# Moving 56 modulation tiles between the stages of a one-core diffusion/mLSTM layer

## The chip, the core and the metric

The kernel runs on one core of one Trainium2 chip. The metric is the device time of one execution in microseconds (us). A core has five engines that run their own instruction streams in order and wait for each other by semaphores: PE (matmul; its weight loads are shown apart as PEld), DVE (VectorE), ACT (ScalarE), POOL (GpSimd) and SP (SyncE, used here only to issue transfers). An instruction at the head of a stream that waits for something holds up everything behind it in that stream.

## The reference

One layer over 128 context tokens and 512 latent tokens (T = 640, width D = 1024) in fp32. Nine modulation vectors per conditioning row come from one small product; every other step uses some of them:

```python
def adaln(cvec, w, b):                       # w (D, 9*D); two rows: c_ctx and c
    m = jax.nn.silu(cvec) @ w + b
    return m.reshape(cvec.shape[0], N_MOD, D_MODEL)

def layer(x, mods, l, p, ctx):
    hh = rmsnorm(x, g[0]) * (1 + m[1]) + m[0]
    x = x + 0.5 * m[2] * swiglu(hh, ffn1_w1, ffn1_w3, ffn1_w2)     # first half-step
    hh = rmsnorm(x, g[1]) * (1 + m[4]) + m[3]
    y, ctx_out = token_mixer(hh, p, l, ctx)                        # attention || mLSTM
    x = x + m[5] * y
    hh = rmsnorm(x, g[2]) * (1 + m[7]) + m[6]
    x = x + 0.5 * m[8] * swiglu(hh, ffn2_w1, ffn2_w3, ffn2_w2)     # second half-step
```

`token_mixer` projects `hh` to everything at once, normalises and rotates the attention's queries and keys, runs differential softmax attention with 8 heads, and a chunkwise mLSTM with 4 heads in both directions (5 chunks of 128 tokens, with a matrix state C that each chunk updates); each branch is gated and both are projected out.

## The kernel before, in words

Everything is kept feature-major: x is 8 tiles of 128 features by 640 tokens, handled as two halves of 320 tokens (`hf` 0 and 1). fp32 products are made from three products of split operands: a high part (names ending in H) and the remainder (L). A weight tile arrives as `raw`, ACT copies it to the H part, and DVE subtracts to get the L part (L123 and L39 in attention and mLSTM, L283/L265 and L39 in the half-steps, whose tiles are called `wB`, `wC` and `ww`). PE cannot start on a weight tile before DVE's subtraction is done. The weights' `raw` tiles come from a ring of two buffers.

The stages, in order: a start in which m0 and m1 are made on PE; the first half-step (up-projections, then down-projections in 28 products numbered `i`; each product has places `at` = 0 and 1 between its parts); the second norm; projections of q, k, v with rotation; attention, head by head (`hd` 0 to 7), each in five score steps (`qi` 0 to 4); the mLSTM, head by head, in ten cells each (five chunks, two directions); the output projection; the second half-step. Independent projections ("fill units" of 24 matmuls each, `Fill`) are threaded between the dependent steps of attention and mLSTM to keep PE occupied.

The modulation vectors m2 to m8 aren't made on PE. They are 56 "tiles", each a 128x1024 piece of the weight that is loaded (512 KB, `raw_a` or `ada`) and multiplied with the two conditioning rows (`csil`, kept replicated on all 128 partitions, 1 MB) and summed along its rows on DVE: two instructions at L626 per tile, one for each row. `Columns.tile()` emits one tile, `Columns.place(n, csil, load)` says from where the next n tiles take their buffers. `columns.then` makes the derived scales when a vector's eight tiles are done. Where the tiles are put is what the change edits:

- in the first half-step `modulation(i, at)` puts one tile at `at` = 1 of products 2 to 17, and one more at `at` = 0 of products 4 and 12 (18 tiles). From product 20 on (the last part of the down phase, which needs no up-projection) there is one at `at` = 0 and two at `at` = 1 of each of eight products (24 tiles); there `csil`, `junk` and the loaded tiles sit in the buffers of tags B and C, those of the weight parts `wB` and `wC`
- in attention the loop over heads puts one tile behind the scores of `qi` 1 and 3 of heads 0 to 5, and one more at `qi` 2 of heads 2 and 4 (14 tiles). `csil` is loaded again there, into the buffers of two later mLSTM operands.

Four other things sit at the places that the change touches. `Stats.add` squares x (`nsq`) on ACT and sums the eight squares into `nacc` on DVE for the second norm; for the second half of the tokens its tag is `nt`, which the norm of the first half (`norm_apply`, `nt`, `hH`, `hL`) uses at that time too. `gate_products` loads and splits the weights of the mLSTM's gates (`wgH` L981, `wgL`), and `gate_rows` turns their product `ps_g` into gate rows. `Head.pack` splits a head's queries (`qpk`, L1160 on ACT, then a subtraction on DVE) and copies its keys (`kpk`, L1164); `queries` then transposes `qpk` on PE (`ps_qkT`) and makes the keys' remainder, and `keys` transposes the keys. The residual x is loaded again at product 18.

The program's text is written once in dependency order; a scheduler at build time orders each engine's instructions, with `tc.issue_after(ins)` as a lower bound on where a block may be put. DMA waits in the stream of SP count: SP issues in order, and a load whose buffer isn't free stands in front of all later loads.

## Time and profile before

| | before |
|---|---|
| time, median of 3 runs | 1912.65 us (1911.35 to 1914.5) |
| the profiled execution | 1915.8 us, of which the profile's span is 1914.0 us |
| PE busy | 1817.3 us, 95% of the span, 12,622 matmuls |
| DVE busy | 1330.7 us, 70% |
| ACT busy | 856.7 us, 45% |
| mean granted TensorE clock | 0.981 |
| moved by DMA | 304.68 MB, 159 GB/s over the span |

"Busy" is the time in which an engine had an instruction in it. A row of the timeline view has the start and duration, the engine, the line and operation, the tiles (out<-in), and in square brackets how long the engine stood idle just before and which instruction ended that wait. The windows view gives the busy time of each engine in a stretch, with the granted clock of TensorE (PEclk; 1.00 is full speed, 0.93 over 25 us means 3.5 us at half speed) and the share of time the DMA engines were busy.

### The profile page before, as it was taken

To read this page: it belongs to the slowest core of one execution; us is meant where nothing else is said; L and a number is where in the kernel's file an instruction comes from. 1 tells how busy PE (TensorE), PEld (TensorE's weight loads), DVE (VectorE), ACT (ScalarE), POOL (GpSimd) and SP (SyncE) were. 2 spreads that over 40 slices of the span, in tenths; PEclk is the share of its full clock that TensorE was granted. 3 is DMA by queue.
4 is the path that set the end of the run, shared out by engine and by line. 5 is a ranking of instruction groups with operands and counts; after the bars stand their busy time and mean duration, and the time that the engine had idled before them with its cause. 6 is when DMAs were issued, how large, how long until landed. Compare 5 with 4: busy or idle time off the path is not lost.

```text
span 1914.0 us, 30831 instructions
## 1 busy us (share of the span) xinstructions
PE 1817.3 (95%) x12622; PEld 1777.5 (93%) x12622; DVE 1330.7 (70%) x2252; ACT 856.7 (45%) x1469; POOL 50.9 (3%) x81
## 2 busy tenths in 40 slices
PE   6899999998989999999999989999999999998989
PEld 4899999997888999999999989899999999998989
DVE  7788987487777566675765545664457888886775
ACT  5644444111454454453544446555335655553332
POOL 1000001010000000000000000000000000001100
PEclk9999999998999999999999999999999999999989
DMA  8344557965414323223121353445432454557952
GB/s 321 116 144 178 181 188 265 376 208 171 153 45 159 102 72 123 76 95 104 68 103 60 107 165 92 144 162 194 176 131 79 169 182 171 179 184 266 355 209 93
DMA packets 129471, 304.68 MB, mean 159 GB/s; under 512 B 9585, under 2 KB 93041, under 8 KB 116657
## 3 DMA queue, kind: packets, MB, share of 16 engines
q1 hardware_dynamic: 115714, 241.04, 36.4%
q0 software_dynamic: 13616, 61.67, 8.7%
q8 instruction: 99, 1.62, 0.4%
q14 instruction: 42, 0.34, 0.1%
HBM read 236.10 MB, written 66.58 MB: 158 GB/s over the span
## 4 chain that ended last, share of the span: by engine, by line
PE 72%; DVE 10%; DMA 9%; issue 3%; ACT 3%; POOL 0%; SPq 0%; DVEq 0%; ACTq 0%; POOLq 0%
PE ps_f L52 29%; PE ps_p L52 21%; PE ps_t L52 11%; PE ps_o L52 2%; PE sc L52 2%; DMA g_dram<-g 2%; DMA raw<-in_w2b 2%; DMA ada<-in_w_ada_c 2%; PE ps_n L52 2%; DVE ww L39 2%; PE ps_wT L55 1%; PE ps_u L52 1%; PE ps_qkT L55 1%; DVE ada L626 1%; DVE junk L626 1%
## 5 line engine op out<-in xcount | busy, mean ns | idle before, releaser
L52 PE MATMUL ps_f<-S,ww 128*128 128x320 f32 x2052 | 333.9, 312 | 10.7 <-DVE ww L39 4.8
L52 PEld LDWEIGHTS ps_f<-S,ww 128*128 128x128 f32 x2052 | 310.9, 190 | 14.0 <-DVE ww L39 7.3
L52 PE MATMUL ps_p<-hH,wH 128*128 128x320 f32 x864 | 274.5, 318 | 3.1 <-ACT aT L1268 2.5
L52 PE MATMUL ps_p<-hL,wH 128*128 128x320 f32 x864 | 267.7, 310 | 0.0
L52 PE MATMUL ps_p<-hH,wL 128*128 128x320 f32 x864 | 267.6, 310 | 0.0
L52 PE MATMUL ps_t<-wH,hH 128*128 128x256 f32 x640 | 186.1, 291 | 0.9 <-DVE x L42 0.9
L52 PE MATMUL ps_f<-hm,wB 128*128 128x320 f32 x1128 | 182.5, 311 | 0.0
L52 PE MATMUL ps_t<-wL,hH 128*128 128x256 f32 x640 | 182.1, 285 | 0.0
L52 PE MATMUL ps_t<-wH,hL 128*128 128x256 f32 x640 | 182.0, 284 | 0.0
L39 DVE TENSOR_TENSOR ww<-raw,ww 128x2048 fp32r<-128x2048 f32 (+1 forms) x62 | 138.7, 2237 | 54.9 <-ACT ww L265 30.6
L52 PE MATMUL ps_f<-hm,ww 128*128 128x320 f32 x996 | 160.2, 313 | 12.5 <-ACT u L375 9.3
L52 PEld LDWEIGHTS ps_f<-hm,wB 128*128 128x128 f32 x1128 | 170.8, 189 | 0.0
L52 PEld LDWEIGHTS ps_p<-hH,wH 128*128 128x128 f32 x864 | 163.3, 189 | 4.3 <-ACT aT L1268 2.7
L52 PEld LDWEIGHTS ps_f<-hm,ww 128*128 128x128 f32 x996 | 151.8, 192 | 13.5 <-ACT u L375 9.9
L52 PEld LDWEIGHTS ps_p<-hL,wH 128*128 128x128 f32 x864 | 163.1, 189 | 0.5
L52 PEld LDWEIGHTS ps_p<-hH,wL 128*128 128x128 f32 x864 | 162.9, 189 | 0.0
L39 DVE TENSOR_TENSOR wL<-raw,wH 128x2048 fp32r<-128x2048 f32 x49 | 112.1, 2288 | 41.5 <-ACT wH L123 41.4
L123 ACT ACTIVATE wH<-raw 128x2048 fp32r<-128x2048 f32 x49 | 93.6, 1911 | 100.2 <-PE ps_p L52 88.7
L265 ACT ACTIVATE ww<-raw 128x2048 fp32r<-128x2048 f32 (+1 forms) x52 | 97.7, 1880 | 84.2 <-PE ps_f L52 53.7
L39 DVE TENSOR_TENSOR raw<-raw 128x1024 f32<-128x1024 f32 (+2 forms) x156 | 132.5, 850 | 1.8
L52 PEld LDWEIGHTS ps_t<-wH,hH 128*128 128x128 f32 x640 | 123.8, 193 | 1.3 <-ACT hH L201 1.1
L52 PEld LDWEIGHTS ps_t<-wL,hH 128*128 128x128 f32 x640 | 123.9, 194 | 0.3 <-issue 0.2
(294 smaller groups left out, 3295.0 us busy)
## 6 DMA issues: line engine op xcount, KB each, us to landing
g_dram<-g SPq DMA_DIRECT2D x44, 640.0 KB, 5.0
ada<-in_w_ada_c POOLq DMA_DIRECT2D x24, 512.0 KB, 4.7
hm<-g_dram POOLq DMA_DIRECT2D x9, 1280.0 KB, 13.0
raw<-in_w1b SPq DMA_DIRECT2D x11, 1024.0 KB, 4.8
raw<-in_w3b SPq DMA_DIRECT2D x11, 1024.0 KB, 4.8
g_dram<-g SPq DMA_DIRECT2D x22, 480.0 KB, 4.2
raw<-in_w1a SPq DMA_DIRECT2D x10, 1024.0 KB, 4.8
raw<-in_w3a SPq DMA_DIRECT2D x10, 1024.0 KB, 7.4
```

The source lines that it names most:

```text
L39: return eng.tensor_tensor(out=out, in0=in0, in1=in1, op=op)
L52: tc.keep_in_program_order(nc.tensor.matmul(*args, **kw))
L55: tc.keep_in_program_order(nc.tensor.transpose(*args, **kw))
L123: act(h, raw, AF.Copy)
L265: act(t[0], flat, AF.Copy)
L626: vec.tensor_tensor_reduce(out=junk, in0=raw, in1=self.csil[:, v, :], op0=ALU.mult, op1=ALU.add, scale=1.0, scalar=0.0, accum_out=mod[:, c ...
```

## The change: what it does

1. The modulation's 56 tiles are dealt out anew: 14 in the up phase (`at` = 1 of products 2 to 15), 18 in the last eight down products (one at each place, and a second at `at` = 1 of products 22 and 25 only), 14 in attention (heads 1 to 5 at `qi` 1 and 3, heads 1 to 4 at `qi` 2; none in head 0), and 10 in the mLSTM, behind the reciprocal of certain cells of heads 0, 1 and 2. For those `csil2`, 1 MB, is loaded once more at the mLSTM's start into a pool of its own ("ada2").
2. The reload of the residual x (2.5 MB) is not touched in the text, but its buffers are those of the up-phase tiles, which end two products earlier: the scheduler now puts it ahead of the last `w3a` tile in SP's stream instead of behind it and behind the first `w2a` loads.
3. The squares of the second half of the tokens get a tag of their own (`nsq`, two buffers).
4. `gate_products` is emitted behind the second half's norm instead of behind its statistics.
5. `Head.pack` is cut in two. Head 0's queries are packed before the fill of v begins, into the pool "gates"; its keys are packed where both were packed before. Head 0's `gate_rows` must now also follow the copies of its keys on ACT.

```diff
@@ class Stats, add @@
-            tag, bufs = ("nt", 2) if self.n < KT else (("nrv", 1), ("nsq", 2))[self.hf]
+            tag, bufs = ("nsq", 2) if self.hf else ("nt", 2) if self.n < KT else ("nrv", 1)
@@ first half-step @@
-        columns.place(18, csil, load_columns)
+        columns.place(14, csil, load_columns)
...
             if i < 20:
-                if 2 <= i < 18 and (at or i % 8 == 4):
+                if at and 2 <= i < 16:
                     columns.tile(hs.at_vec)
...
-                    columns.place(24, csil, load_columns)
+                    columns.place(18, csil, load_columns)
                 columns.tile(hs.at_vec)
-                if at:
+                if at and i in (22, 25):
                     columns.tile(hs.at_vec)
@@ class Head @@
         def pack(self):
+            self.pack_queries(ap, 2)
+            self.pack_keys()
+
+        def pack_queries(self, pool, bufs):
 
             hs = slice(self.h * 128, (self.h + 1) * 128)
             qv = q_tok[self.pr][:, :, hs].rearrange("p t (c d) -> p t c d", c=2)
-            kv = self.kv = k_tok[self.pr][:, :, hs].rearrange("p t (c d) -> p t c d", c=2)
-            self.qpk = ap.tile([128, 5, 4, 64], F32R, tag="pk", name="qpk", bufs=2)
+            self.qpk = pool.tile([128, 5, 4, 64], F32R, tag="pk", name="qpk", bufs=bufs)
             act(self.qpk[:, :, 0::3, :], qv, AF.Copy)
             tt(vec, self.qpk[:, :, 1:3, :], qv, self.qpk[:, :, 0::3, :].bitcast(F32), ALU.subtract)
+
+        def pack_keys(self):
+            hs = slice(self.h * 128, (self.h + 1) * 128)
+            kv = self.kv = k_tok[self.pr][:, :, hs].rearrange("p t (c d) -> p t c d", c=2)
             self.kpk = ap.tile([128, 5, 4, 64], F32R, tag="pk", name="kpk", bufs=2)
             for i in range(2):
-                act(self.kpk[:, :, i::2, :], kv, AF.Copy)
+                self.at_act = act(self.kpk[:, :, i::2, :], kv, AF.Copy)
@@ second norm, projections @@
     with tc.issue_after(stats[1].at_act.ins), tc.issue_after(stats[1].at_vec.ins):
         w_k = split_w(src_k)
-        ps_g, gate_step = gate_products()
...
     tok_group(psum, [(w_k, 0, e_k), (w_k, 1, e_k)], lambda k: None)
+    with tc.issue_after(box["normed"]):
+        ps_g, gate_step = gate_products()
...
+    heads = [Head(hd) for hd in range(8)]
+    gates = ExitStack()
     tok_group(psum, [(w_q, i, e_q) for i in (2, 3, 4)], lambda k: None)
     tok_group(psum, [(w_k, i, e_k) for i in (2, 3, 4)], lambda k: None)
...
+    gt = gates.enter_context(tc.tile_pool(name="gates", bufs=1))
+    heads[0].pack_queries(gt, 1)
...
-        heads[0].pack()
+        heads[0].pack_keys()
         heads[0].queries()
...
-        with tc.issue_after(heads[0].at_vec.ins):
+        with tc.issue_after(heads[0].at_vec.ins), tc.issue_after(heads[0].at_act.ins):
             gate_rows(gt, ps_g)
@@ attention @@
-            if hd < 6 and qi in (1, 3) or (hd, qi) in ((2, 2), (4, 2)):
+            if hd in range(1, 6) and qi in (1, 3) or hd in range(1, 5) and qi == 2:
                 columns.tile()
@@ mLSTM @@
     ml = ExitStack()
+    ada = ExitStack()
+    ada_p = ada.enter_context(tc.tile_pool(name="ada2", bufs=1, side="right"))
+    csil2 = ada_p.tile([128, 2, D], F32, name="csil")
+    nc.sync.dma_start(out=csil2, in_=csil_dram.partition_broadcast(128))
+    columns.place(10, csil2, load_columns, 1)
...
-        for st, then in zip(steps, later):
+        for n, (st, then) in enumerate(zip(steps, later)):
...
             m.cell(*st)
+            if n in ((3, 6, 8), (1, 3, 6, 8), (1, 4, 7), ())[h]:
+                columns.tile(m.at_vec)
...
         m.stats()
+    ada.close()
     fill.drain()
```

The scheduler moves more than the text does, so three places are shown as the engines get them (no times: only the order of the instructions). First DVE near the end of the first half-step's down products. `ISA ada,mod<-ada` is half a modulation tile; the row `mod` behind it reads its sum; `wB` is the weight part that the last part of the down products waits for. Before:

```order
L42 SCALAR_TENSOR_TENSOR x<-ps_f,half_m,x 128x192
L42 SCALAR_TENSOR_TENSOR x<-ps_f,half_m,x 128x128
L626 ISA ada,mod<-ada 128x1024
L626 ISA mod 128x1
L39 TENSOR_TENSOR nacc<-nacc,nsq 128x320
L626 ISA ada,mod<-ada 128x1024
L626 ISA mod 128x1
L39 TENSOR_TENSOR wB<-raw,wB 128x1024 x2
L42 SCALAR_TENSOR_TENSOR x<-ps_f,half_m,x 128x320
L39 TENSOR_TENSOR ww<-raw,ww 128x1536
```

and with the change:

```order
L626 ISA ada,mod<-ada 128x1024
L626 ISA mod 128x1
L39 TENSOR_TENSOR wC<-raw,wC 128x512
L626 ISA ada,mod<-ada 128x1024
L626 ISA mod 128x1
L39 TENSOR_TENSOR wB<-raw,wB 128x1024
L42 SCALAR_TENSOR_TENSOR x<-ps_f,half_m,x 128x192
L42 SCALAR_TENSOR_TENSOR x<-ps_f,half_m,x 128x128
L39 TENSOR_TENSOR mod<-mod,b_ada 128x16
L39 TENSOR_TENSOR wB<-raw,wB 128x1024
L42 SCALAR_TENSOR_TENSOR x<-ps_f,half_m,x 128x192
L42 SCALAR_TENSOR_TENSOR x<-ps_f,half_m,x 128x128
```

Twelve tile passes fewer stand ahead of the two `wB`; they still come behind the last pass, and two more outputs (`x<-ps_f`, a pair of rows or one row each) now follow them before the first `nacc`.

Then ACT where the attention's projections end (`sw`, `kpk`: keys; `qpk`, `qT`: queries; `v_tok`: results of fill units; `fg`, `ig`, `e`: gate rows). Before:

```order
L1005 ACTIVATE e<-fg 64x640
L1140 ACTIVATE v_tok<-ps_t 128x256
L1006 ACTIVATE e<-e 64x640
L159 ACTIVATE rt<-rv 128x20
L1007 ACTIVATE e<-e 64x640
L160 ACTIVATE ry<-rt 128x20
L1140 ACTIVATE v_tok<-ps_t 128x256
L1092 ACTIVATE sw<-k_tok 128x1024
L1160 ACTIVATE qpk<-q_tok 128x5x2x64
L1181 ACTIVATE qT<-ps_qkT 128x2x256 x2
L1164 ACTIVATE kpk<-k_tok 128x10x64 x2
```

and with the change:

```order
L1140 ACTIVATE v_tok<-ps_t 128x256
L1163 ACTIVATE qpk<-q_tok 128x5x2x64
L159 ACTIVATE rt<-rv 128x20
L160 ACTIVATE ry<-rt 128x20
L1140 ACTIVATE v_tok<-ps_t 128x256
L1188 ACTIVATE qT<-ps_qkT 128x2x256 x2
L1188 ACTIVATE qT<-ps_qkT 128x2x128
L1092 ACTIVATE sw<-k_tok 128x1024
L1140 ACTIVATE v_tok<-ps_t 128x256 x2
L1171 ACTIVATE kpk<-k_tok 128x10x64 x2
L1002 ACTIVATE fg<-ps_g,b_g 64x320
```

The queries' copy moves ahead of everything that belongs to the keys, the gate rows move behind the keys, and the keys' copies now stand behind the results of two more fill units.

Last SP's transfers at the start of the mLSTM (`P`, `va`, `C`, `mask` are its first operands). Before:

```order
L74 DMA raw<-in_w_gd 128x2048
L1337 DMA gm_dram<-stage 128x320 x4
L1269 DMA aT_dram<-aT 128x640
L74 DMA raw<-in_w_gm 128x2048
L74 DMA mask<-in_mask 128x256
L1496 DMA va<-v_dram 128x5x256
L1501 DMA P<-nm_dram 128x5x128 x2
```

and with the change:

```order
L74 DMA raw<-in_w_gm 128x2048
L1349 DMA gm_dram<-stage 128x320 x4
L1276 DMA aT_dram<-aT 128x640
L74 DMA raw_a<-in_w_ada_c 128x1024
L1491 DMA csil<-csil_dram 128x2048
L74 DMA mask<-in_mask 128x256
L1512 DMA va<-v_dram 128x5x256
L1517 DMA P<-nm_dram 128x5x128 x2
```

Where one weight tile of 1 MB stood ahead of the operands, there is now one modulation tile of 0.5 MB and the 1 MB of `csil`, and the weight tiles' place in the queue is one load later. PE's instructions are the same in kind, number and order in both programs.

More of the change, by code (lines that the diff above doesn't have):

```diff
@@ L1338, in gate_evac @@
         return f
-    heads = [Head(hd) for hd in range(8)]
-    with tc.tile_pool(name="gates", bufs=1) as gt:
+    with gates:
         src_v, e_v = project_v(0)
@@ L1567, in cell @@
             stt(den, num[:, 256:257], -1.0, den, ALU.mult, ALU.max)
-            vec.reciprocal(den, den)
+            self.at_vec = vec.reciprocal(den, den)
             if accumulate:
```

## The prediction, made before the changed kernel ran

> **What bounds the kernel now.** I read the head of the page first, then the chain of waits, then every gap of PE over a quarter of a microsecond in its timeline, and last the windows around those gaps.
>
> ```profile
> PE 1817.3 (95%) x12622; PEld 1777.5 (93%) x12622; DVE 1330.7 (70%) x2252; ACT 856.7 (45%) x1469; POOL 50.9 (3%) x81
> ...
> PE 72%; DVE 10%; DMA 9%; issue 3%; ACT 3%; POOL 0%; SPq 0%; DVEq 0%; ACTq 0%; POOLq 0%
> ```
>
> PE works 1817.3 of 1914.0 us and carries 72% of the chain. So only two things can move the end, as long as PE's own work stays what it is: the 97 us in which PE stands idle, and the stretches in which its clock is halved behind such a gap. The nine gaps that lie where the change edits something:
>
> ```profile
> 140.92 0.73 PE L52 MATMUL ps_f<-S,ww 128*128 128x320 f32 x2 [2.29 <-DVE ww L39]
> 244.97 0.41 PE L52 MATMUL ps_f<-S,ww 128*128 128x320 f32 x1 [2.56 <-DVE ww L39]
> 349.65 0.41 PE L52 MATMUL ps_f<-hm,ww 128*128 128x320 f32 x1 [1.55 <-DVE ww L39]
> 365.54 0.41 PE L52 MATMUL ps_f<-hm,ww 128*128 128x320 f32 x1 [1.55 <-DVE ww L39]
> 468.79 0.90 PE L52 MATMUL ps_f<-S,wB 128*128 128x320 f32 x2 [8.24 <-ACT wB L283]
> 470.39 0.63 PE L52 MATMUL ps_f<-S,wB 128*128 128x320 f32 x1 [0.69 <-DVE wB L39]
> 512.16 0.81 PE L52 MATMUL ps_ss<-nacc,ones 128*128 128x320 f32 x2 [3.45 <-DVE nacc L39]
> 560.37 0.75 PE L55 MATMUL ps_qkT<-identr,qpk 128*128 128x128 f32 x4 [5.93 <-DVE qpk L39]
> 605.90 0.66 PE L55 MATMUL ps_wT<-ident,p 128*128 128x128 f32 x2 [4.51 <-DVE p L42]
> ```
>
> Eight of these nine rows name DVE as releaser; at 468.79 the wait ended on ACT, whose `wB` had itself waited for DVE (shown below). DVE's 70% is an average; what it does in these stretches, and the clock there:
>
> ```profile
> 125.00:150.00 25.00, 22.71 (x144) 22.45 (x144) 22.31 (x31) 10.16 (x14) 1.59 (x3) 0.93 0.56 197
> 228.00:253.00 25.00, 22.33 (x151) 21.80 (x150) 22.93 (x29) 10.36 (x15) 1.59 (x3) 1.00 0.59 200
> 460.00:485.00 25.00, 16.07 (x89) 15.40 (x88) 18.28 (x31) 8.57 (x11) 0.53 (x1) 0.80 0.47 159
> 500.00:525.00 25.00, 20.69 (x145) 19.82 (x144) 19.93 (x45) 13.22 (x28) 0.00 (x0) 0.93 0.52 176
> 545.00:570.00 25.00, 19.07 (x146) 18.87 (x145) 20.14 (x30) 12.00 (x23) 0.00 (x0) 0.86 0.11 38
> 595.00:620.00 25.00, 20.49 (x138) 19.80 (x137) 16.44 (x26) 7.40 (x12) 0.00 (x0) 0.93 0.62 202
> 1125.00:1150.00 25.00, 19.25 (x120) 17.53 (x120) 10.44 (x26) 13.50 (x37) 0.00 (x0) 1.00 0.73 238
> 1200.00:1225.00 25.00, 23.68 (x138) 21.27 (x136) 18.33 (x56) 14.62 (x39) 0.00 (x0) 1.00 0.65 203
> ```
>
> In 125 to 150 and 228 to 253 DVE is busy 22.3 and 22.9 of 25 us; in the mLSTM (1200 to 1225) 18.3, the fullest of its windows that I looked at. A mean clock of 0.93 is 3.5 us at half speed, so up to 1.75 us lost; 0.80 is 10 us, 0.86 is 7 us, in both of which PE was partly idle anyway. One modulation tile costs DVE two passes:
>
> ```profile
> L626 DVE CUSTOM_DVE_ANT_0 ada<-ada x48: 1211/1220/1228, 334.2 to 468.0; 128x1024 bf16<-128x1024 f32 x48
> ...
>   DMA ada<-in_w_ada_c: 9.7, 10
> ```
>
> The first row is a pass of DVE, 1.22 us, 2.45 us a tile with its partner; the second says that ten passes of these 24 tiles waited for their load, 9.7 us together. The 56 tiles stay 56, so DVE's sum doesn't change; only where it falls does.
>
> **The change, part by part.** Gains are counted against the profiled execution (1915.8 us), which lies 3.15 us over the median of 1912.65; at the end I take them off the median.
>
> *Up phase.* The extra tiles of products 4 and 12 go. The gaps at 140.92 (2.29) and 244.97 (2.56) are at just these two products, and at no other product does DVE's `ww` come late by more than 1.6 us. Taking 2.45 us of DVE away from a wait of 2.29 and 2.56 us removes 2.29 and at least 2.45. The half-speed stretch behind the first is worth 1.7 us; behind the second there is none (1.00). Gain 6.5, between 4.7 (clock unchanged) and 6.6. [...]
>
> *Residual.* Its 2.5 MB move out of the stretch before 349.65, where DVE's `ww` waited for ACT and ACT for a loaded `raw`, into one with DMA to spare. There are two gaps of 1.55 us of this kind (349.65 and 365.54). Gain 2.5, between 0 and 3.1.
>
> *Last down products.* Six tiles fewer, 14.7 us of DVE. How the gap of 8.24 + 0.69 us came about:
>
> ```profile
> 467.97 1.22 DVE L626 CUSTOM_DVE_ANT_0 ada<-ada 128x1024 bf16<-128x1024 f32 x1
> 469.11 2.44 DVE L39 TENSOR_TENSOR wB<-raw,wB 128x1024 fp32r<-128x1024 f32 x2
> 469.23 1.06 ACT L283 ACTIVATE wB<-raw 128x1024 fp32r<-128x1024 f32 x1 [0.49 <-DVE mod L626]
> ```
>
> `wB` sits in the buffer in which `csil` lay, so it can't begin before the very last pass, at 467.97 + 1.22. Taking six tiles off an engine that is nearly full there ends the last pass some 14.7 us earlier, near 454.5; ACT's 1.06 us and DVE's half of 2.44 us put `wB` at about 457, before PE is out of work at 468.79 − 8.24 = 460.55. Both gaps go, and of the 10 us at half speed the some 6 us in which PE worked: 8.9 + 3.0 = 11.9. Bounds: 12; and 6, if the loads of the tiles (and not DVE) set the pace, so that only some of the 14.7 us arrive.
>
> *Second norm.* PE waited 3.45 us at 512.16 for the last `nacc`:
>
> ```profile
> 508.40 1.04 ACT L981 ACTIVATE wgH<-wg_raw 128x1024 fp32r<-128x1024 f32 x1
> 509.83 2.28 DVE L39 TENSOR_TENSOR nacc<-nacc,nsq 128x320 f32<-128x320 f32 x4 [2.72 <-ACT nsq L181]
> ```
>
> The four sums of the second half were made in a row (2.28 us) after the gate weights' copy (1.04) had kept ACT from the squares. With buffers of their own the squares come with each output of x, and the sums among them; DVE is full there (19.93 of 25), and four sums of 0.57 us now delay x itself, by up to 1 us. Gain 3.45 + 1.75 − 0.8 = 4.4, between 1.5 and 5.2.
>
> *Head 0's queries.* PE waited 5.93 us at 560.37 for `qpk`, with 2.0 us of clock behind it:
>
> ```profile
> 549.79 1.22 DVE L39 TENSOR_TENSOR q_tok<-q_tok,sw 128x1024 f32<-128x1024 f32 x1
> 559.49 0.82 DVE L39 TENSOR_TENSOR qpk<-q_tok,qpk 128x640 fp32r<-128x640 f32 x1
> 557.09 0.72 ACT L1160 ACTIVATE qpk<-q_tok 128x640 fp32r<-128x640 f32 x1
> 562.15 1.36 ACT L1164 ACTIVATE kpk<-k_tok 128x640 fp32r<-128x640 f32 x2
> 568.70 0.37 PE L55 MATMUL ps_qkT<-identr,kpk 128*128 128x128 f32 x3
> ```
>
> The rotated queries were done at 549.79 + 1.22 = 551.0 at the latest, but ACT's copy (0.72) came at 557.09 behind the gate rows, and DVE's subtraction (0.82) at 559.49 behind the whole rotation of the keys. With both ahead, `qpk` is ready by about 553.4; PE wants it at 554.44. But what is late next? In the new order ACT's copies of the keys (1.36 us) stand behind the results of two more fill units, and PE wants the keys 8.33 us after the queries (568.70 − 560.37), 6.3 without the halved clock: at 560.8. The second of those results exists only then; 0.4 us for it and 1.36 us for the copies give 562.6, and DVE's chain for the keys (about 7.6 us of passes from 553.4) asks for 561.1. So a gap of some 1.8 us returns, too short by most rows to halve the clock. Gain 5.93 + 2.0 − 1.8 = 6.1, between 2 (a gap of 4 with its clock) and 7.9.
>
> *No tile in head 0.* PE waited 4.51 us at 605.90 for the probabilities `p`; DVE had stood 6.40 us at two tiles' `csil`:
>
> ```profile
> 599.58 1.22 DVE L626 CUSTOM_DVE_ANT_0 raw_a<-raw_a,csil 128x1024 bf16<-128x1024 f32 x1 [6.40 <-DMA csil<-csil_dram]
> ```
>
> Now the first tile comes one score step later and alone, behind the maximum of the next scores. Its passes still stand ahead of that step's `p`, but `csil` will have landed or nearly so. Gain 4.51 + 1.45 clock − 0.5 = 5.4, between 3 and 6.
>
> *Rest of attention.* Heads 2 and 4 keep their three tiles. Head 3 gets a third:
>
> ```profile
> 819.13 1.02 DVE L42 SCALAR_TENSOR_TENSOR p<-p,r,p 128x768 f32<-128x768 f32 x1
> 821.15 0.27 PE L55 MATMUL ps_wT<-ident,p 128*128 128x128 f32 x1
> ```
>
> There `p` is done at 820.15 and PE wants it at 821.15: 1.0 us of slack against 2.45 of passes. Loss 1.2 (half of it lies behind `p`), from 0 to 2.4. Head 1's third tile has over 3 us of slack at its step: 0.
>
> *Start of the mLSTM.* Before, 1 MB of weights stood ahead of `mask`, `va`, `P` and `C`; now 1.5 MB do. PE's first `ps_n` already waits for `P`:
>
> ```profile
> 1143.60 0.70 PE L52 MATMUL ps_n<-va,P 128*128 128x258 f32 x2 [0.89 <-DVE P L39]
> P<-nm_dram SPq DMA_DIRECT2D x4, 320.0 KB, 7.4
> ```
>
> At the 238 GB/s of that window 0.5 MB takes 2.1 us, and `csil` adds a transfer's start. Loss 2.5, from 0 to 5 (1 MB more in the way, and the clock).
>
> *Ten tiles in the mLSTM.* 24.5 us of DVE spread over some 110 us, in which DVE is busy 14 to 18 of 25. No tile was there, so the price must come from the nearest rows: the weight splits `wL`, as long as one tile:
>
> ```profile
> 1167.87 2.29 DVE L39 TENSOR_TENSOR wL<-raw,wH 128x2048 fp32r<-128x2048 f32 x1 [3.97 <-ACT wH L123]
> ...
> 1201.87 2.29 DVE L39 TENSOR_TENSOR wL<-raw,wH 128x2048 fp32r<-128x2048 f32 x1
> 1222.42 0.48 PE L52 MATMUL ps_u<-wv,mktok 128*128 128x258 f32 x1 [1.32 <-ACT Cn L1560]
> ```
>
> The second stands ahead of an update of C, and still PE had no gap of over 0.25 us until 1221.10: the 1.32 us there, which end on ACT, are all its idle time in 1200 to 1225. Cells of the two directions alternate, and fill units of 24 matmuls lie between. A tile is two passes of 1.22 us with cell work between them, kinder than `wL`. From below a tile costs 0; from above all its 2.45 us (24.5). I take 0.4 each, near the `wL` row: 4.
>
> Sum: 6.5 + 2.5 + 11.9 + 4.4 + 6.1 + 5.4 = 36.8 gained, 1.2 + 2.5 + 4 = 7.7 lost, net 29.1. Profiled 1886.7; as a median 1912.65 − 29.1 = **1883.5, say 1884**.
>
> **Rivals.**
>
> *The mLSTM turns DVE-bound* (slower). If each tile holds up the update of C or P that the next cell needs, and each of these gaps halves the clock for a stretch (1.7 us), a tile costs 2.45 + 1.7 = 4.15 us, the ten 41.5: 29.1 + 4 − 41.5 = −8.4, 1921 us. It decides from 3.3 us a tile. For it: DVE at 18.3 of 25, and PE's order is fixed. Against: the `wL` rows.
>
> *The gaps move instead of going.* The two largest terms rest on what is late next. If the tiles' loads hold DVE up in the last down products, and the keys come 4 us late with a halved clock, the terms 11.9 and 6.1 shrink to 4 and 2, and the residual's and the norm's together (6.9) to 2: 1884 + 17 = 1901. For it: the 9.7 us in which DVE waited for loads of tiles. Against: that is 0.4 us a tile.
>
> *The ring of two raw buffers.* In the mLSTM a tile's 0.5 MB take one of the weights' two buffers until its passes are done, so three weight tiles are loaded later than before, just ahead of their split, and DVE, in order, stands still for the load:
>
> ```profile
> raw<-in_w1b SPq DMA_DIRECT2D x11, 1024.0 KB, 4.8
> ```
>
> Three times 4.8 us: 1884 + 14.4 = 1898. Against: two splits lie 34 us apart (1167.87 and 1201.87), and a load, ACT's copy and the split need under 10.
>
> **How the numbers follow.** My forecast 0.68 (own range 1875 to 1893), gaps that move 0.15 (1901), the ring 0.10 (1898), DVE-bound mLSTM 0.07 (1921). The range 1874 to 1906 takes in the two middle cases and leaves out the last and the tails. About 0.2% (3.8 us) is what a measurement here tells from no change: faster 0.89, within 0.04, slower 0.07, the last almost all from the DVE-bound mLSTM.
>
> **What would show it.** Right: no PE gap over 1 us at products 4 and 12, none at the `wB` near 457, `ps_ss` under 1 us, `qpk` gone with about 1.8 us at the keys, no wait for `csil` in head 0, and clock windows only where gaps are left. Wrong: gaps before `ps_u` or `ps_n` in the mLSTM that end on DVE and sum to over 10 us; a DVE idle row there that ends on a load or on ACT's `wH`; or PE at `wB` still waiting for DVE's `mod`.

## The result, and where the time went

The changed kernel takes 1887.3 us (median of 4 runs, 1883.35 to 1888.76), beside 1913.45 us (4 runs, 1911.35 to 1914.5) for the kernel before: ratio 0.9859, 95% interval 0.9843 to 0.9875, or 26.2 us less. Timed again (`after_again`) it was 1888.38 beside 1915.43, ratio 0.9863 (0.9838 to 0.9887). The forecast was 1884, its range 1874 to 1906. The sum was nearly right. Two of its terms were not, and they erred in opposite directions.

The head of the page and the chain of waits of the changed kernel:

```profile
PE 1812.6 (96%) x12622; PEld 1774.3 (94%) x12622; DVE 1329.4 (70%) x2252; ACT 854.6 (45%) x1469; POOL 45.9 (2%) x71
...
PE 82%; DVE 8%; DMA 6%; ACT 2%; issue 1%; SPq 0%; DVEq 0%; ACTq 0%
```

PE is busy for about as long (1812.6 us; 1817.3 before), and its share of the chain rose from 72% to 82%, while DVE's fell from 10 to 8, that of DMA from 9 to 6 and "issue" from 3 to 1. PE's idle time, counted up to its last instruction, fell from 93.2 to 70.5 us. These are the gaps of PE that are left or new where the change edits something, from the timeline of PE:

```profile
359.38 0.57 PE L52 MATMUL ps_f<-hm,ww 128*128 128x320 f32 x2 [2.13 <-DVE ww L39]
540.76 0.54 PE L55 MATMUL ps_qkT<-identr,kpk 128*128 128x128 f32 x4 [1.72 <-ACT kpk L1171]
565.75 0.55 PE L55 MATMUL ps_wT<-ident,p 128*128 128x128 f32 x3 [1.75 <-DVE p L42]
573.04 0.69 PE L52 MATMUL ps_o<-v_tok,wT 128*128 128x128 f32 x2 [2.00 <-DVE wT L1247]
1116.53 0.58 PE L52 MATMUL ps_st<-mqT,mkT 128*128 128x128 f32 x1 [3.40 <-ACT mktok L1535]
1119.88 0.77 PE L52 MATMUL ps_n<-va,P 128*128 128x258 f32 x1 [2.14 <-issue]
```

The gaps at products 4 and 12 and at `wB` are gone, and so are the one at `ps_ss` and the one at head 0's queries. There is now one at head 0's keys (540.76), two in head 0 (565.75, 573.04), and at the start of the mLSTM 3.40 + 2.14 us where there were 1.42 + 0.97 + 0.89. The windows around the same places, with their columns as in the prediction (PE, weight loads, DVE, ACT, POOL, clock, DMA share, GB/s):

```profile
440.00:465.00 25.00, 25.00 (x173) 25.00 (x172) 17.06 (x31) 8.54 (x11) 0.00 (x0) 1.00 0.49 168
550.00:575.00 25.00, 21.26 (x139) 20.38 (x138) 23.79 (x41) 10.37 (x19) 0.00 (x0) 0.96 0.33 108
1110.00:1135.00 25.00, 19.46 (x106) 17.30 (x105) 13.43 (x37) 16.67 (x44) 0.00 (x0) 0.86 0.61 189
1165.00:1190.00 25.00, 25.00 (x157) 23.25 (x156) 22.43 (x68) 11.53 (x33) 0.00 (x0) 1.00 0.39 117
```

Three readings. In 440 to 465, where the last down products now fall, PE is full and DVE at 17.06. In 550 to 575, head 0's first score steps, DVE is at 23.79 of 25 and PE at 21.26, although no tile is left there. And in 1165 to 1190, with tiles in the mLSTM, PE is at 25.00 of 25 with DVE at 22.43. For the second, the same steps of head 0 in the kernel before, where DVE had 15.82:

```profile
590.00:615.00 25.00, 20.49 (x139) 19.89 (x138) 15.82 (x27) 8.46 (x16) 0.00 (x0) 0.93 0.51 156
```

PE executes the same instructions in the same order in both programs, so the start of one and the same instruction in the two traces tells what each part gained. Each row below ends with one such instruction; the difference of the starts, less that of the row above, is the part's share. The last column has the same shares from the trace of `after_again`, the changed kernel profiled a second time.

| part, up to the PE instruction that starts | before | after | difference | share | forecast | share in `after_again` |
|---|---|---|---|---|---|---|
| start of the program, not edited | 90.55 | 92.18 | +1.63 | +1.6 | 0 | +1.0 |
| up phase | 345.88 | 340.95 | -4.93 | -6.6 | -6.5 | -6.5 |
| residual | 368.87 | 362.71 | -6.16 | -1.2 | -2.5 | +0.2 |
| last down products | 479.59 | 461.27 | -18.32 | -12.2 | -11.9 | -12.2 |
| second norm | 533.10 | 511.06 | -22.03 | -3.7 | -4.4 | -3.7 |
| head 0's queries and keys | 580.03 | 553.05 | -26.98 | -5.0 | -6.1 | -6.4 |
| no tile in head 0 | 650.03 | 622.85 | -27.18 | -0.2 | -5.4 | -1.8 |
| rest of attention | 1125.10 | 1098.88 | -26.23 | +1.0 | +1.2 | +2.1 |
| start of the mLSTM | 1152.47 | 1130.07 | -22.40 | +3.8 | +2.5 | +5.1 |
| ten tiles in the mLSTM | 1300.16 | 1275.11 | -25.06 | -2.7 | +4 | -2.0 |
| later, not edited | 1905.04 | 1877.64 | -27.40 | -2.3 | 0 | -3.2 |

The shares sum to 27.4 us; the spans differ by 27.1 (1914.0 and 1886.9). The first and last rows are parts that nobody edited: what differs there is mostly the clock (13.7 us at half speed in the first 70 us before, 20.5 after; behind 1700 us 20.5 before, 17.1 after). So 1 to 2 us of any share can be of that kind, and the last column shows the same: both traces end 27.4 us earlier, with single shares up to 1.6 us apart. In head 0 the two have the same gaps, but in the first a half-speed stretch (573.19 to 576.60) follows the gap of 2.00 us, and in the second none; without it the share is 1.8 us, as in all eight other traces here that leave head 0 as the change has it.

### The profile page after: what moved, and what is told of

Same layout as the page of the kernel before. It is cut to its first block, busy times and chain, and to the rows that moved or that the text cites. A ratio compares the mean times of both kernels' runs of the same rounds, so it can differ in the third digit from the quotient of the medians.

```text
span 1886.9 us, 30810 instructions
## 1 busy us (share of the span) xinstructions
PE 1812.6 (96%) x12622; PEld 1774.3 (94%) x12622; DVE 1329.4 (70%) x2252; ACT 854.6 (45%) x1469; POOL 45.9 (2%) x71
## 4 chain that ended last, share of the span: by engine, by line
PE 82%; DVE 8%; DMA 6%; ACT 2%; issue 1%; SPq 0%; DVEq 0%; ACTq 0%
PE ps_f L52 36%; PE ps_p L52 22%; PE ps_t L52 12%; PE sc L52 2%; PE ps_o L52 2%; PE ps_n L52 2%; DMA raw<-in_w2b 2%; DMA ada<-csil_dram 2%; DVE ww L39 1%; PE ps_u L52 1%; PE ps_wT L55 1%; PE ps_qkT L55 1%; DVE x L42 1%; DVE raw L39 1%; DMA raw_a<-in_w_ada_c 0%
## 5 line engine op out<-in xcount | busy, mean ns | idle before, releaser
L52 PEld LDWEIGHTS ps_t<-wH,hL 128*128 128x128 f32 x640 | 123.7, 193 | 0.5 <-DVE hL L42 0.5
```

The source lines that it names most:

```text
L52: tc.keep_in_program_order(nc.tensor.matmul(*args, **kw))
```

## The experiments

Each is an edit of the changed kernel, timed beside the kernel before on the same chip. The kernel before has medians of 1915.43 to 1916.34 us beside these, 1913.45 in the first comparison, so ratios are compared, to the change's own 0.9859 and 0.9863.

### Are the three large terms due to what was named?

`up_extra` puts the tiles of `at` = 0 in products 4 and 12 back (16 tiles there, 8 in the mLSTM):

```diff
-                if at and 2 <= i < 16:
+                if 2 <= i < 16 and (at or i % 8 == 4):
```

> The changed kernel with the extra tiles of products 4 and 12 put back into the up phase (16 tiles there) and two fewer in the mLSTM (8, none behind cells 4 and 7 of head 2). Theory (each gap belongs to its own tile): PE gaps of about 2.3 and 2.6 us come back at just these two products, +5 us without and +6.5 us with a halved clock behind the first: 1892 to 1894 us. Rival (the up phase only got better because two tiles' loads went off its queues, wherever they sat): no gap over 1 us there, 1887 us. Rival (the mLSTM's tiles cost something): up to 5 us of this is given back by the two tiles less in head 2.

1890.73 us, ratio 0.9875 (0.9859 to 0.9891). Both gaps come back with the very lengths they had:

```profile
141.09 0.57 PE L52 MATMUL ps_f<-S,ww 128*128 128x320 f32 x1 [2.29 <-DVE ww L39]
245.16 0.56 PE L52 MATMUL ps_f<-S,ww 128*128 128x320 f32 x2 [2.56 <-DVE ww L39]
```

In the time that is some 3 us, less than the 5 to 6.5 expected. In the trace it is 5.1 us behind the changed kernel by product 12 (6.5 if the 1.4 us that its start happened to be quicker are added back), and gains 2.8 at the residual, whose 2.13 us gap at `ww` is missing in this run. That gap comes and goes: in the kernels here with the change's up phase it is 2.23 us in one, 1.23 or 0.52 in others, and absent in `no_passes`, which differs from the change only 800 us later. In DVE's timeline three passes of tiles stand ahead of that `ww`, and the first of them waits for `csil`, the copy that the down products load: 14.92 us in the changed kernel, 12.3 to 15.3 in the edited ones. So the two tiles cost what was forecast, and the gain of 2.8 isn't theirs for certain.

`down24` gives the last down products their 24 tiles again (4 in the mLSTM):

```diff
-                if at and i in (22, 25):
+                if at:
```

> The changed kernel with 24 tiles in the last eight down products as before, and only 4 in the mLSTM (cells 3 and 8 of heads 0 and 1). Theory (the number of tiles keeps DVE from wB): the gap before the last wB comes back with 8 to 9 us and a halved clock, +11 to 12 us: 1898 to 1900 us. Rival (the earlier reload of the residual, which stays in this kernel, has freed the loads and the tiles run sooner): a gap of 3 to 5 us, 1891 to 1894 us.

1902.24 us, ratio 0.9930 (0.9913 to 0.9946); the trace ends 13.1 us later than the change's. The two gaps at `wB` return, and with them 10.24 us of half clock (455.24 to 465.48); 11.3 of the 13.1 us arise in this part.

```profile
460.22 0.63 PE L52 MATMUL ps_f<-S,wB 128*128 128x320 f32 x1 [7.97 <-ACT wB L283]
462.00 0.64 PE L52 MATMUL ps_f<-S,wB 128*128 128x320 f32 x1 [0.88 <-DVE wB L39]
```

`nsq_back` takes the squares' own buffers away, and `gatew_back` emits `gate_products` at its old place:

```diff
-            tag, bufs = ("nsq", 2) if self.hf else ("nt", 2) if self.n < KT else ("nrv", 1)
+            tag, bufs = ("nt", 2) if self.n < KT else (("nrv", 1), ("nsq", 2))[self.hf]
```

```diff
         w_k = split_w(src_k)
+        ps_g, gate_step = gate_products()
```

> The changed kernel with the old tag for the squares of the second half of the tokens. Theory (the shared buffer puts the four last sums behind the first half's norm): the gap at the second norm's ps_ss comes back with 2.5 to 3.5 us, with its clock +4 to 5 us: 1891 to 1892 us. Rival (the gate weights' copy ahead of the squares was the cause; here it is after them): a gap of under 1.5 us, 1887 to 1889 us.

> The changed kernel with the gate weights' products emitted where they were before, behind the statistics instead of behind the norm. Theory (the squares' own buffers alone remove the norm's gap): no PE gap over 1 us at ps_ss, 1886 to 1889 us. Rival (ACT's copy of the gate weights, 1.04 us, and DVE's subtraction, 1.22 us, hold up the squares and the norm): a gap of 1 to 2.5 us there, 1889 to 1892 us. Since their load takes one of the two raw buffers earlier, the scheduler orders the tiles of the last down products otherwise; if that matters, the gap before wB grows from 0 and the time with it.

The first took 1891.19 us, ratio 0.9873 (0.9859 to 0.9887), with the old gap back at the sums of the norm:

```profile
494.77 0.54 PE L52 MATMUL ps_ss<-nacc,ones 128*128 128x320 f32 x1 [3.19 <-DVE nacc L39]
```

The gap is 3.19 us, but this part of the trace is only 1.9 us longer than in the changed kernel, and no half-speed stretch follows: the buffers account for 1.9 of the 3.7 us, and the 1.7 us of clock that stood behind the gap before (half speed from 513.19 to 516.61) is the rest. The second took 1887.25 us, ratio 0.9855 (0.9840 to 0.9869), with no gap at `ps_ss`, and this part of its trace is 0.3 us longer than the change's. The place of `gate_products` is worth next to nothing here; the gap belongs to the buffers.

### Head 0: a changed order, or a full DVE?

Taking the tiles out of head 0 removed the wait for `csil` and the gap of 4.51 us, and gained 0.2 us (1.8 in `after_again`). This is what DVE does now ahead of the two gaps of head 0 (its timeline):

```profile
562.08 2.57 DVE L1028 TENSOR_TENSOR_SCAN lf<-keep,m,u 4x512 f32<-4x512 f32 x2
564.68 1.02 DVE L42 SCALAR_TENSOR_TENSOR p<-p,r,p 128x768 f32<-128x768 f32 x1
...
570.36 2.29 DVE L39 TENSOR_TENSOR wL<-raw,wH 128x2048 fp32r<-128x2048 f32 x1
572.57 0.42 DVE L1247 COPY wT<-ps_wT 128x256 f32<-128x256 f32 x1
```

The first `p` stands behind the long scan of the gate rows, and `wT` behind a weight split. In the kernel before the same scan was done twelve us before PE wanted its first `wT`, by DVE's timeline and PE's:

```profile
576.36 2.58 DVE L1028 TENSOR_TENSOR_SCAN lf<-keep,m,u 4x512 f32<-4x512 f32 x2
```

```profile
590.81 0.60 PE L55 MATMUL ps_wT<-ident,p 128*128 128x128 f32 x4
```

576.36 + 2.58 = 578.94, and 590.81 follows with no gap; now the scan ends at 562.08 + 2.57 = 564.65, and PE has been out of work since 565.75 - 1.75 = 564.0. The question was why. One theory blames the new order: the gate rows wait for ACT's copies of the keys, start late and so meet head 0's `p`. The other says that DVE has more to do between the queries and the second score step than PE leaves time for, so that an order only chooses where PE waits. Three kernels tell these apart: `pack_back` packs queries and keys together again, `rows_free` lets the gate rows start without the keys' copies, `rows_split` holds DVE's part of the gate rows back until head 0's first `p`.

```diff
@@ pack_back @@
-    heads[0].pack_queries(gt, 1)
...
-        heads[0].pack_keys()
+        heads[0].pack()
@@ rows_free @@
-        with tc.issue_after(heads[0].at_vec.ins), tc.issue_after(heads[0].at_act.ins):
+        with tc.issue_after(heads[0].at_vec.ins):
@@ rows_split @@
-            gate_rows(gt, ps_g)
+            rest = gate_rows(gt, ps_g)
         fill.one()
         heads[0].scores(0)
+        with tc.issue_after(heads[0].at_p.ins):
+            rest()
```

> The changed kernel with head 0's queries packed where they were before, together with its keys; the gate rows stay behind the keys. In the changed kernel's trace the 5.93 us gap before the queries' transposes is gone, but 1.72 us before the keys' (ACT kpk), with a halved clock, and 1.75 and 2.00 us with another halved clock in head 0's first steps are new. Theory A (the packing removed the gap, and the keys' gap is its follow-up): the gap at the queries comes back with 5 to 6 us and its clock, the one at the keys goes; head 0's two stay: +3 to 5 us against the changed kernel. Theory B (the whole chain from the rotation to the first scores is DVE-bound, so a gap removed at one place comes back at the next): head 0's two gaps shrink as well, and the time stays within 1.5 us of the changed kernel.

> The changed kernel without the wait of the gate rows for the copies of head 0's keys, so that ACT makes the gate rows ahead of the queries' copy, as before the change; the packing stays apart. Theory A (the gate rows, moved behind the keys, now stand between the first scores and their p, and that makes head 0's two new gaps): the 1.75 and 2.00 us gaps go or shrink to under 1 us and a gap of 0.5 to 1.5 us appears at the queries: -2 to -4 us against the changed kernel. Theory B (some 15 us of gate rows on DVE have no room between the keys and the first p, wherever they start): the sum of the gaps in head 0 stays between 3 and 5 us: within 1.5 us.

> The changed kernel with the gate rows' DVE part (scans and what follows) held back until the p of head 0's first scores is done. Theory A and B of the run before agree that the first gap (1.75 us before the first transposes of p) goes. A: the rows then share DVE with one more score step that has slack, the second gap (2.00 us, wT behind a weight split) shrinks too: -2 to -5 us against the changed kernel. B (DVE has no room in any of the first steps): the gap only moves one step on, to the p of the second scores, with 2 to 4 us: within 1.5 us, or slower.

Their gaps of over 1 us from the queries to the end of head 0, in the timelines of PE of the three in turn:

```profile
534.83 0.62 PE L55 MATMUL ps_qkT<-identr,qpk 128*128 128x128 f32 x3 [4.55 <-DVE qpk L39]
566.66 0.55 PE L55 MATMUL ps_wT<-ident,p 128*128 128x128 f32 x3 [1.09 <-DVE p L42]
579.95 0.52 PE L55 MATMUL ps_wT<-ident,p 128*128 128x128 f32 x3 [2.63 <-DVE p L42]
```

```profile
541.37 0.54 PE L55 MATMUL ps_qkT<-identr,kpk 128*128 128x128 f32 x4 [1.72 <-ACT kpk L1171]
567.81 0.55 PE L55 MATMUL ps_wT<-ident,p 128*128 128x128 f32 x3 [3.19 <-DVE p L42]
581.20 0.52 PE L55 MATMUL ps_wT<-ident,p 128*128 128x128 f32 x3 [2.74 <-DVE p L42]
```

```profile
537.76 0.54 PE L55 MATMUL ps_qkT<-identr,kpk 128*128 128x128 f32 x4 [1.72 <-ACT kpk L1174]
567.14 0.60 PE L52 MATMUL ps_o<-v_tok,wT 128*128 128x128 f32 x3 [2.58 <-DVE wT L1250]
575.96 0.55 PE L55 MATMUL ps_wT<-ident,p 128*128 128x128 f32 x3 [1.66 <-DVE p L42]
```

`pack_back` has 4.55 + 1.09 + 2.63 = 8.3 us of gaps, and takes 1889.25 us, ratio 0.9860 (0.9847 to 0.9874). `rows_free` has 1.72 + 3.19 + 2.74 = 7.7: without the wait that the first theory blames, the gap at head 0's first `p` grew from 1.75 to 3.19; 1891.06 us, ratio 0.9868 (0.9854 to 0.9881). `rows_split` has 2.58 + 1.66 = 4.2 beside the keys' 1.72: the gap at the first `p` is gone, but the next one grew from 2.00 to 2.58, and 1.66 follows at the second score step; 1889.99 us, ratio 0.9859 (0.9845 to 0.9873). None of these times is apart from the change's.

The last gap of `pack_back` and that of `rows_free` are not of this kind. There the scheduler moved the first modulation tile of attention into head 0, and its passes wait for `csil` ahead of `p`, as in the kernel before (DVE, `pack_back` and then `rows_free`):

```profile
575.65 1.23 DVE L626 CUSTOM_DVE_ANT_0 raw_a<-raw_a,csil 128x1024 bf16<-128x1024 f32 x1 [4.38 <-DMA csil<-csil_dram]
577.41 1.23 DVE L626 CUSTOM_DVE_ANT_0 raw_a<-raw_a,csil 128x1024 bf16<-128x1024 f32 x1 [3.48 <-DMA csil<-csil_dram]
```

Without these two, the gaps are 5.6 us in `pack_back`, 4.9 in `rows_free`, 6.0 in `rows_split` and 5.5 in the changed kernel: four orders, and nearly the same sum. The first theory, that the wait for the keys' copies makes the gaps, falls with `rows_free`. The second fits, but it is argued, not shown, since no run here leaves the gate rows out. It has a limit too: DVE is full only in part of the stretch (23.79 of 25 in 550 to 575, but 39.28 of 50 in 532 to 582), so what binds is its passes between fixed points of PE, not its sum over the whole, and a better order than these four isn't excluded. Packing apart is the plainest sign: of the 4.55 us that it took away at the queries, 1.72 came back at the keys and 2.66 in head 0 (1.75 + 2.00 instead of 1.09).

### The mLSTM: what the tiles and their start cost

`no_passes` leaves out the twenty DVE passes of the ten tiles, with a memset in their place, and keeps the loads (so ten columns of the modulation stay zero). `double` makes each of these passes twice.

```diff
@@ no_passes @@
+                if skip:
+                    vec.memset(mod[:, ct, :], 0.0)
-                for v in range(2):
+                for v in range(0 if skip else 2):
@@ double @@
-                for v in range(2):
+                for v in (0, 1, 0, 1) if twice else range(2):
```

> The changed kernel without the DVE passes of the mLSTM's ten tiles: their loads and csil's stay, each tile's sums are set to zero instead (a part of m7 and all of m8 are left out, so the output is not the reference's). Theory (the passes lie wholly in DVE's idle time there): no PE gap goes, within 1.5 us of the changed kernel. Rival (each tile costs PE something, as the forecast's 0.4 us a tile has it): -3 to -5 us.

> The changed kernel with the passes of the mLSTM's ten tiles made twice (four passes of 1.22 us a tile, 24.5 us of DVE more in that stage). Theory (what counts is how long DVE is away from the cells at a time, and two pairs with cell work between them still fit): 0 to 3 us more. Rival (DVE is close to its limit in the mLSTM, 18 of 25 us before): once the slack is used up every further pass is paid in full, 10 to 24 us more, with PE gaps before ps_n or ps_u that end on DVE.

Without the passes: 1889.58 us, ratio 0.9864 (0.9841 to 0.9886), no faster than with them. Two gaps stand there that the changed kernel doesn't have, ahead of the same two PE instructions as in the kernel before (0.30 us, and 1.32 at 1222.42):

```profile
1161.78 0.70 PE L52 MATMUL ps_u<-wv,mktok 128*128 128x258 f32 x2 [0.87 <-ACT stage L1350]
1198.32 0.70 PE L52 MATMUL ps_u<-wv,mktok 128*128 128x258 f32 x2 [1.47 <-ACT Cn L1578]
```

With the passes twice: 1900.98 us, ratio 0.9929 (0.9907 to 0.9952), 12.6 us over the change on the same chip. Most of it is one gap and the clock behind it (0.86 in 1215 to 1240). DVE works through that gap without a break, with three passes of tiles (from 1216.34, 1217.81 and 1219.16) ahead of the `hs` that PE waits for. Shown are 25 us earlier in that stage in which DVE is full, the 11 us that hold the gap, and the gap's own row (windows, then PE's timeline):

```profile
1165.00:1190.00 25.00, 24.54 (x155) 22.84 (x154) 24.93 (x75) 11.63 (x33) 0.00 (x0) 1.00 0.33 103
1210.00:1221.00 11.00, 3.76 (x20) 2.54 (x20) 10.99 (x26) 4.91 (x13) 0.00 (x0) 0.93 0.37 112
```

```profile
1220.93 0.66 PE L55 MATMUL ps_hT<-ident,hs 128*128 128x128 f32 x2 [6.38 <-DVE hs L42]
```

So the first 24.5 us of DVE in the mLSTM cost nothing, and the second 24.5 cost half of themselves: the DVE-bound mLSTM of the rivals, one more dose away. A full window isn't the bound by itself, since with DVE at 24.93 of 25 in 1165 to 1190 PE still worked 24.54; what cost was passes in DVE's queue ahead of the very result that PE's next matmul waits for. Why the ACT-ended gaps are absent when tiles stand there was not settled: with the passes DVE comes later to the updates, and whatever ACT then finds in its queue isn't shown by these traces.

`csil_late` issues the 1 MB of `csil2` behind the mLSTM's first operands instead of ahead of them; `after_again` is the changed kernel once more, for the comparison.

```diff
-    nc.sync.dma_start(out=csil2, in_=csil_dram.partition_broadcast(128))
...
     mem[0].load()
     mem[0].load_c()
+    nc.sync.dma_start(out=csil2, in_=csil_dram.partition_broadcast(128))
```

> The changed kernel with the second load of csil (1 MB) issued behind the mLSTM's first operands (mask, va, P, C) instead of ahead of them. In the changed kernel PE waits 3.40 and 2.14 us at the start of the mLSTM, 5.5 in all with a halved clock behind, against 3.3 us and no halved clock before. Theory (csil in front of P and C is what makes the start later): 2 to 3.5 us of gaps there, no halved clock, -2 to -5 us against the changed kernel. Rival (the modulation tile and the weights ahead of them, or ACT's share of the start, set it): the gaps stay at 4.5 us or more, within 1.5 us. The first tile's passes come 4 to 5 us behind the operands; if csil is then late for cell 3, a wait of DVE at its first pass shows it.

> The changed kernel itself, unedited, as the partner of the three runs beside it. Expected: its ratio to the kernel before again, 0.986 +- 0.002, and the same PE gaps to a tenth of a microsecond in the middle of the kernel.

`csil_late`: 1884.02 us, ratio 0.9827 (0.9811 to 0.9843). `after_again`: 1888.38, 0.9863 (0.9838 to 0.9887), with the gaps of the middle of the program within 0.1 us of the first trace, except one in head 4 (1.86 us instead of 2.32), and 3.45 + 2.69 at the start of the mLSTM. SP's queue in the changed kernel, then in `csil_late`, and PE's one gap there:

```profile
1105.20 0.32 SPq L1491 DMA_DIRECT2D csil<-csil_dram  x1
1106.05 0.54 SPq L1512 DMA_DIRECT2D va<-v_dram  x1
1106.63 3.53 SPq L1517 DMA_DIRECT2D P<-nm_dram  x2
...
1110.19 2.36 SPq L74 DMA_DIRECT2D C<-in_c_aug  x1
```

```profile
1103.75 0.54 SPq L1511 DMA_DIRECT2D va<-v_dram  x1
1104.34 1.70 SPq L1516 DMA_DIRECT2D P<-nm_dram  x2
1106.08 3.21 SPq L74 DMA_DIRECT2D C<-in_c_aug  x2
1109.33 0.43 SPq L1643 DMA_DIRECT2D csil<-csil_dram  x1
```

```profile
1114.66 0.58 PE L52 MATMUL ps_st<-mqT,mkT 128*128 128x128 f32 x1 [4.04 <-ACT stage L1348]
```

In the changed kernel `P` sits 3.53 us in issue behind `csil`, and `C` follows at 1110.19; with `csil` behind, `P` takes 1.70 and `C` goes at 1106.08. PE waits 4.04 us instead of 3.40 + 2.14. Those 1.5 us are what the trace can show. The ratios differ by 0.0032, some 6 us with an uncertainty of about 4, and the rest of that isn't in this stage: the trace of `csil_late` was already 1.8 us ahead at 1100, with one stretch of half clock fewer. And the sum of the gaps at this start varies by itself, 3.67 us in `gatew_back` and 5.75 in `nsq_back`, neither of which touches it. What speaks for the queue is the whole part: from the end of attention to the end of the table's row "start of the mLSTM" PE takes 30.0 us in `csil_late` and 27.7 in `best` below, which also has `csil` behind, and 30.95 to 32.7 in the eleven traces with `csil` ahead. The direction is clear, the size is not.

`best` adds to `csil_late` a dealing of the tiles that takes three more out of attention, (2, 1), (4, 1) and (3, 2), into the mLSTM (13 there), to remove the gaps of 1.42, 0.79 and 2.32 us at 718, 789 and 857.

```diff
-    columns.place(14, csil, load_columns, 1)
+    columns.place(11, csil, load_columns, 1)
...
-            if n in ((3, 6, 8), (1, 3, 6, 8), (1, 4, 7), ())[h]:
+            if n in ((3, 6, 8), (1, 3, 5, 6, 8), (1, 3, 4, 6, 8), ())[h]:
```

> A version that puts the findings together: the changed kernel with csil's second load behind the mLSTM's first operands, and three attention tiles (the qi 1 tiles of heads 2 and 4, and the qi 2 tile of head 3, behind which PE waits 1.42, 2.32 and 0.79 us) moved to the mLSTM (13 tiles there, also behind cells 5 of head 1, and 1, 3, 4, 6 and 8 of head 2). Theory (tiles are free in the mLSTM and not in attention): the three attention gaps go with one halved clock, no gap comes in the mLSTM: -4 to -6 us for these and -2 to -4 us for csil, -6 to -10 us against the changed kernel. Rival (attention's gaps are the weight split's, not the tile's): only csil's part, -2 to -4 us.

1882.90 us, ratio 0.9832 (0.9808 to 0.9856): it can't be told from `csil_late`, so moving the three tiles shows no gain of its own. Of the three gaps only the one of 0.79 us went. At the other two the scheduler put another tile there instead. At the first its pass waits 1.32 us for its load ahead of the same `p` (DVE, then PE):

```profile
714.03 1.23 DVE L626 CUSTOM_DVE_ANT_0 raw_a<-raw_a,csil 128x1024 bf16<-128x1024 f32 x1 [1.32 <-DMA raw_a<-in_w_ada_c]
715.18 1.01 DVE L42 SCALAR_TENSOR_TENSOR p<-p,r,p 128x768 f32<-128x768 f32 x1
```

```profile
716.25 0.55 PE L55 MATMUL ps_wT<-ident,p 128*128 128x128 f32 x3 [1.72 <-DVE p L42]
```

With 13 tiles there is still no gap that ends on DVE among the mLSTM's cells, although DVE is busy for 24.21 of 25 us in 1200 to 1225; one of 0.99 us that ends on ACT is new.

## Why the prediction was right, and where it was not

**Right, with their sizes.** *Up phase* (6.5; 6.6 in the trace, and both gaps back in `up_extra`), *last down products* (11.9; 12.2, and +11.3 us in `down24`), *second norm* (4.4; 3.7, of which `nsq_back` returned 1.9 and not the clock). In the first two the work on DVE ahead of the awaited part was the cause, and taking that much of it off DVE took the gap away. In the third it was the shared buffer, and DVE's work stayed the same. The step "not DVE but the loads set the pace" of the middle rival didn't come about.

**Mis-sized.** *Residual*: 2.5 forecast, 1.2 measured, and a loss of 0.2 in `after_again`. The two gaps of 1.55 became one of 2.13 at 359.38, still on `ww` but behind passes that wait for `csil`, and this one isn't in every run. *Head 0's queries*: 6.1 forecast, 5.0 measured. The gap of 5.93 went and one of 1.72 came at the keys, 1.8 forecast; but the text took it for too short to halve the clock, and it did, for 3.4 us. In `after_again` it did not, and the part gained 6.4. *Start of the mLSTM*: a loss of 2.5 forecast, 3.8 measured, inside its bounds of 0 to 5 (5.1 in `after_again`, at their edge); `csil_late` and `best` say that the queue ahead of `P` is part of it.

**Wrong: the step "No tile in head 0".** It let 4.51 us of gap and 1.45 us of clock go, less 0.5, and 0.2 us came (1.8 in `after_again`): gaps of 1.75 and 2.00 us stand where 4.51 stood. What it missed is what the prediction itself asked for elsewhere: if a stall goes, what is late next? Before, the last of DVE's passes for the gate rows (`ig`, at 587.0) ended 3.0 us ahead of PE's first `wT`; with the gate rows behind the keys, as ACT's order listing has it, that pass ends 8.5 us behind it (574.3 beside 565.75), so that these passes now lie in 550 to 575, among head 0's first score steps. DVE was full there without tiles, and three other orders of the same work gave 4.9 to 6.0 us of gaps, the two that a tile made set aside. The row for it was in the trace of before, and was not used: the scan at 576.36, and how long before PE's first `wT` it was done. That the gate rows and not some other work of DVE are what has no room is argued from these rows. Between them, the steps *Head 0's queries* and *No tile in head 0* promised 11.5 and gave 5.2 (8.2 in `after_again`); both rest on the same DVE, and each was worked out as though the other's work weren't there.

**Wrong in sign: the step "Ten tiles in the mLSTM".** 4 us of loss forecast, 2.7 gained in the trace (2.0 in `after_again`). That the passes cost nothing is shown (`no_passes`), and that `wL` was the right neighbour to go by: it cost nothing either. The small gain, three gaps of 1.32 us or less that ended on ACT and are absent now, isn't explained. Neither the ring of two raw buffers nor the DVE-bound mLSTM came about; `double` shows how near the second is.

So 1884 came close because a gain of 5.2 that did not come and a loss of 6.7 that did not come either stood against each other, with 1 to 1.3 us each at the queries, the residual and the start of the mLSTM. That these two cancelled was luck. The range was wide enough for the sum, but the own range of each of these two terms (3 to 6, and 0 to 24.5 lost) did not hold what was measured.

## What to carry to other kernels

Two edits that relieve the same in-order engine in neighbouring places are one term, not two: add up what that engine must do between the two points at which its consumer is fixed, and compare with the time the consumer leaves; if it doesn't fit, reordering mostly picks where the wait shows (4.9 to 6.0 us in four orders here). For work that may lie anywhere, the window view gives the place: a stretch where the consumer is full and the engine has 7 us of 25 to spare took all ten tiles for nothing. Read the queue order that the change really gives: the gaps that went here were those where what stood ahead of the awaited instruction went, and a scheduler can put another tile into the place that was cleared, as in `pack_back`, `rows_free` and `best`.

## What the runs showed of the hardware

The half-speed stretches in the traces of the kernel before and of the changed kernel last 3.41 us or multiples of it (6.83, 10.24), apart from the one that the program's end cuts short, and the length of a gap alone doesn't say whether one follows. Before, the 2.29 us at product 4 are followed by one of 3.41 us (141.14 to 144.55), the 2.56 us at product 12 by none (a clock of 1.00 in 244.97 to 248.40). The gap at head 2's queries is 2.46 us in both programs. This is its row in the changed kernel, and then the 3.3 us behind it before and the 3.2 us behind it with the change:

```profile
682.09 0.54 PE L55 MATMUL ps_qkT<-identr,qpk 128*128 128x128 f32 x4 [2.46 <-DVE qpk L39]
```

```profile
709.40:712.70 3.30, 3.30 (x31) 3.30 (x31) 1.99 (x3) 2.61 (x5) 0.00 (x0) 1.00 0.00 0
```

```profile
682.50:685.70 3.20, 3.20 (x20) 3.20 (x19) 1.82 (x3) 2.64 (x5) 0.00 (x0) 0.50 0.00 0
```

The gap of 1.72 us at head 0's keys is followed by half a clock in the changed kernel and by a full one in `csil_late`, whose text is the same up to there (windows of both, 3.4 us long and as far behind the gap):

```profile
542.50:545.90 3.40, 3.40 (x18) 3.40 (x18) 3.15 (x10) 2.34 (x4) 0.00 (x0) 0.50 0.02 5
```

```profile
542.20:545.60 3.40, 3.40 (x33) 3.40 (x32) 3.18 (x10) 3.32 (x6) 0.00 (x0) 1.00 0.02 5
```

So, in these traces, a gap of 1.7 to 2.5 us has its 1.7 us of clock in one place or run and not in another. In the changed kernel half speed begins behind these gaps at 542.47, 573.19 and 682.41. What decides whether a stretch follows was not shown. The forecast's question, whether a gap is long enough to halve the clock, so has only a chance as its answer before the run, worth up to 1.7 us for a gap of this length; in a profile it can be read off.
